# A list scheduler's table of durations corrected from a trace, in an fp32 network kernel on one core

## The chip, the cores and the metric

The kernel runs on one core of a Trainium2 chip. The metric is the device time of one execution in microseconds (us). A change of about 0.2% (6 us here) is the least that a measurement of this kernel can tell from none.

## The reference, cut to what matters

The input is one sequence of 512 tokens of width 1024, all in float32. Two blocks follow each other. The first has an "even" layer (a 31-tap convolution branch and an RWKV-7 recurrence) and an "odd" layer (attention over the best 128 keys per query). The second has a convolution and pooling mixer, a mixture of 16384 one-row experts (PEER), and a gate. The change bears most on PEER:

```python
s = einsum('thpd,hpkd->thpk', q, sub_keys)         # routing: 8 heads, two halves
sv, si = top_k(s, 16)
top_s, pos = top_k(cand, 16)                       # 16 experts per token and head
eidx = take_along_axis(cidx, pos, axis=-1)
gate = softmax(top_s)
u = take(expert_u, eidx, axis=0)
act = gelu(einsum('thkd,td->thk', u, xb))
v = take(expert_v, eidx, axis=0)
out = einsum('thk,thkd->td', gate * act, v)
```

## The kernel before, in words

Matrix products are made in float32r, as three products of a high and a low part (`product`, L216 to L218): high by high, high weight by low input, low weight by high input. A weight piece is loaded by a transfer that SyncE (SP) issues, ScalarE (ACT) makes its high part (`wh`, L207), and GpSimd (POOL) subtracts it to get the low part (`wl`, L209). In the even layer the low part is made by an adding transfer that GpSimd issues instead (`dl`, L192).

PEER (`peer`, L1182 on) works in three stretches.

- **Routing** (`route`, L1399 on). Eight heads of scores, top-16 searches on VectorE (DVE). Then the *scatter*: for 352 of the 512 tokens, eight at a time (44 steps), the chosen gates are spread over all 16384 experts. A step makes one-hot tiles on VectorE (`o`, L1519, and `ob`, L1522), scales them on ScalarE (L1527) and GpSimd (L1528), multiplies them on TensorE (PE, L1533), and copies the result to `st` (L1536). Eleven stores bring `st` to a table `gs` in HBM (L1537).
- **u products.** One tile per 128 experts: activations times expert_u, through gelu (`u_phase`, L1196 to L1199). Thirty-two of the 128 tiles are made ahead, beside the routing, and kept in HBM (`ga`). A u tile is 8 blocks of three matmuls with 352 columns.
- **V stretch** (L1216 on). For each 128 experts `g4`, a piece of the table, is read (L1227), multiplied with the u tile (L1234), split, and multiplied with expert_v (L1264 to L1266), whose low part `vl` GpSimd makes for six tiles of eight (L1248).

The other 160 tokens take another way: 320 *gathers*, indirect transfers that GpSimd issues (`grow`, L1338), one row of 1024 floats for each of 128 partitions. The first 160 rows go into dot products on VectorE (L1353), the other 160 into a weighted sum (L1369). A gather may stand anywhere from the routing to the end of the V stretch. Its tile has five buffers.

Buffers are shared in time: tiles of the V stretch may be written only when all of the routing's pools are closed. Among these is `wx`, an extra buffer for raw weights (`wrawx`) that u tiles use as long as the routing lasts.

No order is written by hand. `Order` builds the dependency graph of the program, estimates each instruction (`cost`), and runs a list scheduler over it (`run`) for several priorities; the order with the shortest estimated end is imposed on every engine's queue and on SP's transfers. Every engine then works strictly in that order.

Of the kernel before, what the change touches and what calls it, by code (L numbers as in the profile page):

```python
# [1566 lines left out]
class Order:  # L1567
# [4 lines left out]
    SETS = {"Exp": (0, 6), "Tanh": (0, 2, 18), "Ln": (5, 6), "Silu": (18,), "Sigmoid": (2,), "Sin": (18,),  # L1572
            "Gelu_apprx_tanh": (11,)}
    LOAD, SWITCH, LANES = 1283, 4000, 8
    TICK, BUSY = 10240 / 3, 3060
    SHAPE = 94

    def __init__(self, nc):
# [15 lines left out]
    def cost(self, i):  # L1594

        e, op = str(i.engine).split(".")[1], str(i.opcode)
        ins = [a for a in i.ins if hasattr(a, "ap")]
        out = list(i.outs)

        def size(a):  # L1600
            return math.prod(c for _, c in list(a.ap)[1:])

        def psum(a):
            return self.mem.get(a.memref, ("",))[0] == "PSUM"
        if "DMA" in op and e == "Pool":
            return e, 0, 1038, 0, 4 * math.prod(c for _, c in out[0].ap)
        if "DMA" in op:
            run = min(list(a.ap)[-1][1] if list(a.ap)[-1][0] == 1 else 1 for a in ins + out)
            return e, 0, 450 if run >= 128 else 625, 0, 4 * math.prod(c for _, c in out[0].ap) * (1 if run >= 128 else 2)
        if op == "LoadActFuncSet":  # L1610
            return e, 0, self.LOAD, 0, 0
        n = max([size(a) for a in ins + out])
        if e == "PE":
            n = size(out[0])
            rows, cols = i.tile_size
            self.shape[i.name] = rows, cols
            one = n / 2.4
            self.col[i.name] = n * rows / 128
            if i.tile_position[1]:
                return e, cols / 1.2, 20, 20, 0  # L1620
            p = 2 if i.is_transpose else 1 if str(i.ins[0].dtype).endswith("float32r") and n >= 256 else 4
            self.col[i.name] *= p
            return e, cols / (2.4 if i.is_transpose else 1.2), p * one + 2.5, one, 0
        sc = sum(size(a) == 1 for a in ins) if n > 1 else 0
        big = [a for a in ins if size(a) > 1]
        if e == "Activation":
            acc = len(out) > 1
            return e, 0, n / 1.2 + (51 if psum(ins[0]) else 93) + 93 * (sc + acc), 0, 0
        if e == "DVE":
            if op == "Memset":  # L1630
                return e, 0, n / 0.96 + 8, 0, 0
            fast = op in ("TensorScalarPtr", "TensorCopy") and len(big) < 2 and not any(map(psum, ins))
            return e, 0, (n / (2 if fast else 1) + 66 + 60 * sc) / 0.96, 0, 0
        if op == "Memset":
            return e, 0, n / 1.2 + 36, 0, 0
        return e, 0, n * (2.1 if len(big) > 1 else 3.3) + 150, 0, 0
# [113 lines left out]
    def run(self, pri):  # L1750
        c, use, dep = self.c, self.use, self.dep
# [18 lines left out]
        soon = {e: [] for e in self.HOP}  # L1770
        now = {e: [] for e in self.HOP}
        lanes, cols, ring, dma, array, table, shape = [], {}, 0.0, 0.0, 0.0, None, None
        out = []

        def push(n):
# [5 lines left out]
        def done(n):  # L1781
            wait[n] -= 1
            if not wait[n]:
                push(n)
# [3 lines left out]
        while len(out) < len(self.seq):  # L1788
            t, e = min((free.get(e, 0) if now[e] else max(free.get(e, 0), soon[e][0][0]), e)
                       for e in soon if now[e] or soon[e])  # L1790
            while soon[e] and soon[e][0][0] <= t:
                _, k, n = heapq.heappop(soon[e])
                heapq.heappush(now[e], (-pri[n], k, n))
            if e == "Activation":
                b = min(now[e], key=lambda z: z[0] + (self.SWITCH if self.fn[z[2]] and table not in self.fn[z[2]] else 0))
                now[e].remove(b)
                heapq.heapify(now[e])
                n = b[2]
            elif e == "PE":
                b = min(now[e], key=lambda z: z[0] + (self.SHAPE if self.shape[z[2]] != shape else 0))  # L1800
                now[e].remove(b)
                heapq.heapify(now[e])
                n = b[2]
            else:
                n = heapq.heappop(now[e])[2]
            _, load, d, last, size = c[n]
            if self.fn[n] and table not in self.fn[n]:
                table = self.fn[n][0]
                t += self.LOAD
            start[n] = t  # L1810
            if size and e == "Pool":
                free[e] = t + d + 3
                dma = end[n] = max(dma, t + d + 650) + size / 360
            elif size:
                if len(lanes) >= self.LANES:
                    t = max(t, lanes[-self.LANES] + 900)
                ring = max(t, ring) + d
                dma = max(dma, ring + 650) + size / 360
                free[e], end[n] = ring, dma
                lanes.append(dma)  # L1820
            elif e == "PE":
                k = int(max(array, t) / self.TICK)
                slow = 1 if cols.get(k - 1, 0) >= self.BUSY else 2
                d += self.SHAPE if self.shape[n] != shape else 0
                shape = self.shape[n]
                array = end[n] = max(array, t + load * slow) + d * slow
                free[e] = array - last * slow + 3
                k = int(array / self.TICK)
                cols[k] = cols.get(k, 0) + self.col[n]
            else:  # L1830
                end[n] = t + d
                free[e] = end[n] + 3
            out.append(n)
            for m in self.succ[n]:
                done(m)
            seen = set()
            for tl in holds.get(n, ()):
                tleft[tl] -= 1
                if not tleft[tl] and queue[self.tag[tl]]:
                    w = first[queue[self.tag[tl]].pop(0)]  # L1840
                    extra[w] = max([extra.get(w, 0)] + [end[x] + self.hop(x, w) for x in use[tl]])
                    done(w)
                p = self.mem[tl][3]
                if p not in seen:
                    seen.add(p)
                    pleft[p] -= 1
                    if not pleft[p]:
                        te = max(end[x] for x in members[p]) + 150
                        for q in self.over[p]:
                            for t2 in self.pools[q]:  # L1850
                                w = first[t2]
                                extra[w] = max(extra.get(w, 0), te)
                                done(w)
# [59 lines left out]
```

## Time and profile before

| | |
|---|---|
| time, median of 3 runs | 2848.27 us (2845.97 to 2852.17) |
| the profiled execution's own time | 2844.42 us |
| its span, first to last instruction | 2842.7 us |
| mean granted TensorE clock | 0.965 of 2.4 GHz |
| TensorE busy with matmuls | 2609.6 us, 92% |
| VectorE, GpSimd, ScalarE busy | 2154.0, 1724.6, 1481.2 us |
| read from and written to HBM | 507.76 and 41.42 MB |

The profile is one execution, so a sum of its durations is to be set against 2844.42 us, of which 1.7 us lie outside the span; the median of the runs is 3.9 us above it. Even layer, odd layer and mixer take the first half of the span, PEER runs from about 1400 us to 2766 us, and the last gate follows.

### The profile page before, as it was taken

Reading aid. Unit: us, or ns where it says so; the run is one execution under the profiler, and the core shown is the slowest. Engines: PE = TensorE matmul, PEld = TensorE weight load, DVE = VectorE, ACT = ScalarE, POOL = GpSimd, SP = SyncE. Lnnn points to the kernel's source line nnn. Section 1 sums busy time; section 2 is a strip of 40 time slices with the busy share of each in tenths; the row PEclk is TensorE's granted clock in tenths of the full one; section 3 lists DMA queues with packets and bytes.
Section 4 is the critical chain, followed back from the end, with each engine's and each line's share of the span. In section 5 each row is a group of like instructions: output and inputs, shape, how many; then the busy total and the mean of one; then the engine's idle time right before and its main releaser. Section 6 shows DMA issues by size and latency. Waiting matters only on the chain. (4 is left out here: it accounts for less than half of the span.)

```text
span 2842.7 us, 45654 instructions
## 1 busy us (share of the span) xinstructions
PE 2609.6 (92%) x14715; PEld 2220.0 (78%) x14715; DVE 2154.0 (76%) x4307; ACT 1481.2 (52%) x3177; POOL 1724.6 (61%) x1870
## 2 busy tenths in 40 slices
PE   5889999999798899999999987779999999999996
PEld 3656667666576688887888777779999999999995
DVE  6686669865379998954669999667877787787875
ACT  6646557568455358965353367424334333344435
POOL 4423523222164443346657788779988888899973
PEclk9889899999899999999999999989999999999998
DMA  8744355555872221223334356889999999999972
GB/s 260 172 96 97 82 117 119 103 145 122 216 241 91 71 80 46 71 84 106 92 111 141 107 193 251 293 299 326 338 321 334 334 337 335 309 334 330 336 253 80
DMA packets 353444, 552.27 MB, mean 194 GB/s; under 512 B 60082, under 2 KB 239154, under 8 KB 351539
## 3 DMA queue, kind: packets, MB, share of 16 engines
q1 hardware_dynamic: 224690, 295.22, 32.2%
q0 software_dynamic: 64800, 201.88, 23.9%
q10 hardware_dynamic: 63712, 52.24, 5.8%
q8 instruction: 116, 1.90, 0.3%
q14 instruction: 126, 1.02, 0.1%
HBM read 507.76 MB, written 41.42 MB: 193 GB/s over the span
## 5 line engine op out<-in xcount | busy, mean ns | idle before, releaser
L209 POOL TENSOR_TENSOR wl<-wraw,wh 128x256 fp32r<-128x256 f32 x937 | 748.3, 816 | 395.8 <-ACT wh L207 314.8
L207 ACT ACTIVATE wh<-wraw 128x256 fp32r<-128x256 f32 x937 | 363.0, 411 | 422.0 <-PE mm L217 198.2
L216 PE MATMUL mm<-xh,wh 128*128 128x352 f32 (+1 forms) x1464 | 513.2, 352 | 32.4 <-ACT wh L207 17.4
L218 PE MATMUL mm<-xh,wl 128*128 128x352 f32 (+1 forms) x1464 | 510.6, 352 | 18.8 <-POOL wl L209 18.8
L217 PE MATMUL mm<-xl,wh 128*128 128x352 f32 (+1 forms) x1464 | 510.5, 350 | 2.3 <-DVE xl L287 2.3
L216 PEld LDWEIGHTS mm<-xh,wh 128*128 128x128 f32 x1464 | 280.5, 192 | 57.2 <-ACT wh L207 21.0
L218 PEld LDWEIGHTS mm<-xh,wl 128*128 128x128 f32 x1464 | 280.5, 192 | 42.1 <-POOL wl L209 24.5
L217 PEld LDWEIGHTS mm<-xl,wh 128*128 128x128 f32 x1464 | 280.8, 192 | 23.3 <-DVE xl L287 4.6
L192 POOL DMA_DIRECT2D dl<-in_wev x114 | 100.7, 904 | 284.1 <-ACT dl L191 261.3
L1248 POOL TENSOR_TENSOR vl<-vraw,vh 128x1024 fp32r<-128x1024 f32 x96 | 230.9, 2407 | 4.0 <-ACT vh L1244 3.0
L1369 DVE SCALAR_TENSOR_TENSOR wide<-grow,gdot,wide 128x1024 f32<-128x1024 f32 x158 | 202.4, 1281 | 17.1 <-DMA grow<-in_ev,gidx 15.9
L218 PE MATMUL mm<-xh,dl 128*128 128x512 f32 x456 | 197.0, 436 | 15.5 <-DMA dl<-in_wev 15.5
L1353 DVE SCALAR_TENSOR_TENSOR gscr<-grow,wide 128x1024 bf16<-128x1024 f32 x160 | 194.1, 1213 | 19.4 <-DMA grow<-in_ue,gidx 18.1
L1199 ACT ACTIVATE mm<-mm 128x352 f32<-128x352 f32 x96 | 43.0, 448 | 314.4 <-PE mm L218 308.5
L216 PE MATMUL mm<-xh,dh 128*128 128x512 f32 x456 | 193.4, 428 | 13.0 <-ACT xh L355 12.3
L1338 POOL DMA_INDIRECT grow<-in_ue,gidx x160 | 164.2, 1026 | 57.8 <-DVE gscr L1353 20.2
L217 PE MATMUL mm<-xl,dh 128*128 128x512 f32 x456 | 191.1, 422 | 6.2 <-DVE xl L356 6.2
L1338 POOL DMA_INDIRECT grow<-in_ev,gidx x160 | 162.6, 1016 | 42.8 <-issue 18.1
L1244 ACT ACTIVATE vh<-vraw 128x1024 fp32r<-128x1024 f32 x128 | 134.4, 1054 | 83.2 <-DMA vraw<-in_ev 70.5
L1264 PE MATMUL xu<-wwh,vh 128*128 128x352 f32 x512 | 167.0, 326 | 5.2 <-DVE x L1268 2.6
L1266 PE MATMUL xu<-wwh,vl 128*128 128x352 f32 x512 | 166.1, 326 | 4.6 <-POOL vl L1248 2.6
L1265 PE MATMUL xu<-wwl,vh 128*128 128x352 f32 x512 | 165.8, 324 | 0.0
(582 smaller groups left out, 6818.7 us busy)
## 6 DMA issues: line engine op xcount, KB each, us to landing
vraw<-in_ev SPq DMA_DIRECT2D x128, 512.0 KB, 5.7
wraw<-in_uT SPq DMA_DIRECT2D x494, 128.0 KB, 4.7
draw<-in_wev SPq DMA_DIRECT2D x114, 256.0 KB, 3.4
dl<-in_wev POOLq DMA_DIRECT2D x114, 256.0 KB, 4.7
gs<-st SPq DMA_DIRECT2D x11, 2048.0 KB, 7.7
g<-gs ACTq DMA_DIRECT2D x32, 704.0 KB, 10.3
wraw<-in_wod SPq DMA_DIRECT2D x156, 128.0 KB, 2.2
adaw<-in_adaT SPq DMA_DIRECT2D x32, 512.0 KB, 8.1
```

The source lines that it names most:

```text
L207: nc.scalar.activation(wh, raw[:, s], AF.Copy)
L209: nc.gpsimd.tensor_tensor(wl, raw[:, s], wh.bitcast(F32), OP.subtract)
L216: nc.tensor.matmul(ps, wh, xh, start=start, stop=False)
L217: nc.tensor.matmul(ps, wh, xl, start=False, stop=False)
L218: nc.tensor.matmul(ps, wl, xh, start=False, stop=stop)
L1248: nc.gpsimd.tensor_tensor(l, raw, h.bitcast(F32), OP.subtract)
L1264: nc.tensor.matmul(po, vh[i][:, s], wh[i], start=(i == 0), stop=False)
L1265: nc.tensor.matmul(po, vh[i][:, s], wl[i], start=False, stop=False)
L1266: nc.tensor.matmul(po, vl[i][:, s], wh[i], start=False, stop=(i == len(wh) - 1))
L1338: self.nc.gpsimd.indirect_dma_start(out=t, out_offset=None, in_=src, in_offset=bass.IndirectOffsetOnAxis(ap=self.gidx[i][:, k:k + 1], axis=0))
L1353: nc.vector.scalar_tensor_tensor(scr, u, 1.0, x, op0=OP.mult, op1=OP.mult, accum_out=self.gdot[i][:, k:k + 1])
L1369: nc.vector.scalar_tensor_tensor(acc, r, w, acc, op0=OP.mult, op1=OP.add)
```

## The change

Nothing in the program changes, only `Order`'s estimates, and with them the order in which each engine gets its instructions.

- An adding transfer on GpSimd is taken as 920 ns of issue in place of 1038, and as 10 bytes per element for the transfer engines in place of 4.
- A one-pass matmul costs 15 ns over its columns in place of 2.5.
- VectorE work with two operands in SBUF, or in its fast mode, takes 1.25 times as long per element.
- The model of TensorE's clock gets two thresholds, one to rise and one to fall, and keeps its state between them.

```diff
-    TICK, BUSY = 10240 / 3, 3060
+    TICK, BUSY, FULL = 10240 / 3, 4000, 7200
+    PORT = 1.25
...
-            return e, 0, 1038, 0, 4 * math.prod(c for _, c in out[0].ap)
+            add = str(out[0].dtype).endswith("float32r")
+            return e, 0, 920 if add else 1038, 0, (10 if add else 4) * math.prod(c for _, c in out[0].ap)
...
-            return e, cols / (2.4 if i.is_transpose else 1.2), p * one + 2.5, one, 0
+            return e, cols / (2.4 if i.is_transpose else 1.2), p * one + (15 if p == 1 else 2.5), one, 0
...
-            return e, 0, (n / (2 if fast else 1) + 66 + 60 * sc) / 0.96, 0, 0
+            port = fast or sum(not psum(a) for a in big) > 1
+            return e, 0, (n / (2 if fast else 1) * (self.PORT if port else 1) + 66 + 60 * sc) / 0.96, 0, 0
...
-                slow = 1 if cols.get(k - 1, 0) >= self.BUSY else 2
+                while tick < k:
+                    c2 = cols.get(tick, 0)
+                    slow = (1 if c2 >= self.FULL / 2 else 2) if slow == 2 else 2 if c2 < self.BUSY else 1
+                    tick += 1
```

What this does to the order is spread over the even layer, the start of the odd one, and PEER. Counted in the two orders, on GpSimd's and VectorE's queues:

| | before | changed |
|---|---|---|
| dot products (L1353) ahead of the first one-hot step / of the last | 8 / 16 | 0 / 6 |
| gathers ahead of the last L1528 of the scatter | 21 | 11 |
| gathers ahead of the 1st, 49th, 61st, 79th, 85th `vl` (L1248) | 39, 188, 222, 267, 285 | 23, 168, 205, 266, 285 |
| `wl` (L209) between first and last L1528 | 23 | 36 |
| u blocks on TensorE between first and last L1533 | 35 | 68 |
| u blocks between the last L1533 and the first V matmul | 66 | 28 |

The first place is GpSimd's queue around the end of the scatter; `o0` are the scatter's steps, `grow` gathers, `wl` low parts of expert_u. Before, from the last two steps on:

```order
L1528 TENSOR_TENSOR o0_18738<-ob_18736,kt_18505 128x512
L209 TENSOR_TENSOR wl_19566<-wrawx_19562,wh_19564 128x256
L1528 TENSOR_TENSOR o0_18760<-ob_18758,kt_18505 128x512
L1338 DMA grow_17165<-in_ue,gidx0_14978 128x1024
...
L1338 DMA grow_18952<-in_ue,gidx0_14978 128x1024
L1338 DMA grow_18956<-in_ue,gidx0_14978 128x1024
L209 TENSOR_TENSOR wl_19770<-wrawx_19766,wh_19768 128x256
```

Between the last step and the last use of `wrawx` (`wl_19770`) stand 26 instructions, 13 of them gathers. Now the same `wl_19770` stands ten steps ahead of the last:

```order
L1528 TENSOR_TENSOR o0_18536<-ob_18534,kt_18505 128x512
L209 TENSOR_TENSOR wl_19770<-wrawx_19766,wh_19768 128x256
L1528 TENSOR_TENSOR o0_18558<-ob_18556,kt_18505 128x512
...
L1528 TENSOR_TENSOR o0_18738<-ob_18736,kt_18505 128x512
L1528 TENSOR_TENSOR o0_18760<-ob_18758,kt_18505 128x512
L1338 DMA grow_16287<-in_ue,gidx0_14978 128x1024
L209 TENSOR_TENSOR wl_19908<-wraw_19904,wh_19906 128x256
```

The weights moved ahead of the steps, the gathers behind them. The second place is VectorE's queue at the start of the scatter (`gscr` are dot products, `sel`, `sm` and `top` the end of the routing). Before:

```order
L1353 SCALAR_TENSOR_TENSOR gscr,gdot_14976<-grow,wide 128x1024
L1320 SCALAR_TENSOR_TENSOR gsrc<-sel 128x16 x3
L1322 COPY gidx_14978<-gsrc 128x16 x3
...
L1353 SCALAR_TENSOR_TENSOR gscr,gdot_14976<-grow,wide 128x1024
L1499 TENSOR_REDUCE sm<-sel 128x32
L1353 SCALAR_TENSOR_TENSOR gscr,gdot_14976<-grow,wide 128x1024
L1500 RECIPROCAL sm<-sm 128x32
...
L1353 SCALAR_TENSOR_TENSOR gscr,gdot_14976<-grow,wide 128x1024
L1320 SCALAR_TENSOR_TENSOR gsrc<-sel 128x16 x2
L1519 TENSOR_TENSOR o_17774<-iota,kt 128x1024
```

Now:

```order
L1495 TENSOR_TENSOR sel<-sel,top 128x512
L1322 COPY gidx_14978<-gsrc 128x16
L1320 SCALAR_TENSOR_TENSOR gsrc<-sel 128x16
L1499 TENSOR_REDUCE sm<-sel 128x32
L1500 RECIPROCAL sm<-sm 128x32
L1501 TENSOR_TENSOR sel<-sel,sm 128x512
L1379 COPY gate_17758<-sel 128x128
L1519 TENSOR_TENSOR o_17774<-iota,kt 128x1024
```

The dot products are gone from ahead of the first step. The third place is TensorE's queue in the even layer, at the first triangular solve (L686, 32x32). Before it stands behind projections (`mm<-xh,dh`) and among the next head pair's products (L626):

```order
L216 MATMUL mm<-xh_103,dh 128x512
L217 MATMUL mm<-xl_111,dh 128x512
L218 MATMUL mm<-xh_103,dl 128x512
L686 MATMUL xu<-T_1433,MT 32x32
L626 MATMUL tp<-AR,BK 128x128 x8
L686 MATMUL xu<-T_1433,MT 32x32
L626 MATMUL tp<-AR,BK 128x128 x4
```

Now it stands in one piece among the convolution's products (`uh`, `sg`), ahead of the projections that it stood behind:

```order
L217 MATMUL mm<-sg,pr 128x512
L218 MATMUL mm<-uh,pr 128x512
L216 MATMUL mm<-uh,pr 128x512
L686 MATMUL xu<-T_1433,MT 32x32 x16
L217 MATMUL mm<-sg,pr 128x512
L218 MATMUL mm<-uh,pr 128x512
L644 MATMUL tp<-con,v 128x128 x4
```

Other head pairs' solves and recurrence steps move by about as much, some ahead and some back; from 700 us to 950 us, and from 1200 us to 1500 us, the two orders differ by a few instructions only.

## Rows read from the trace of the kernel before

**Rows 1.** Windows, PEER: length; busy PE, PEld, DVE, ACT, POOL (instructions); clock, DMA share, GB/s.

```profile
1873.00:2440.00 567.00, 553.06 (x3361) 545.44 (x3360) 429.13 (x697) 219.82 (x475) 502.52 (x485) 0.99 0.96 329
2440.00:2600.00 160.00, 157.75 (x974) 156.87 (x973) 128.46 (x163) 66.90 (x138) 144.52 (x136) 1.00 0.94 323
1563.00:1668.00 105.00, 92.29 (x485) 83.14 (x484) 105.00 (x487) 40.17 (x100) 76.29 (x94) 0.94 0.42 130
1668.00:1806.00 138.00, 110.40 (x830) 101.08 (x828) 134.74 (x117) 110.66 (x295) 115.71 (x81) 1.00 0.62 232
1806.00:1873.00 67.00, 41.90 (x201) 38.07 (x201) 29.72 (x48) 16.83 (x41) 42.02 (x49) 0.77 0.92 322
```

**Rows 2.** The chain that ended last, around the start of the V stretch (start us, us).

```profile
1834.86 0.75 POOL wl L209
...
1835.63 0.43 ACTq L1227
...
1836.16 21.08 DMA g<-gs
...
1873.02 0.19 PE xu L1264
```

**Rows 3.** Waits between 1806 and 1873 us: total us, times, longest us.

```profile
PE mm L216 <- ACT wh L207: 15.9, 2, 14.1
PE mm L218 <- POOL wl L209: 9.2, 4, 3.9
```

**Rows 4.** VectorE and GpSimd lines of the routing and gathers: ns min/median/max, first and last start us.

```profile
L1353 DVE SCALAR_TENSOR_TENSOR gscr<-grow,wide x160: 1203/1211/1223, 1644.2 to 2245.6; 128x1024 bf16<-128x1024 f32 x160
L1519 DVE TENSOR_TENSOR o<-iota,kt x44: 1210/1214/3854, 1665.8 to 1802.1; 128x1024 f32<-128x1024 f32 x44
L1522 DVE TENSOR_TENSOR ob<-keys,kb x44: 677/1525/3281, 1666.9 to 1798.4; 128x1024 bf16<-128x1024 bf16 x44
L209 POOL TENSOR_TENSOR wl<-wraw,wh x94: 718/737/1784, 1601.5 to 1900.0; 128x256 fp32r<-128x256 f32 x94
```

**Rows 5.** Groups of the whole span: busy us, mean ns of one, idle before.

```profile
L1519 DVE TENSOR_TENSOR o<-iota,kt 128x1024 f32<-128x1024 f32 x44 | 69.3, 1576 | 0.3 <-PE xu L1533 0.3
L1522 DVE TENSOR_TENSOR ob<-keys,kb 128x1024 bf16<-128x1024 bf16 x44 | 59.5, 1360 | 2.9 <-POOL o L1528 2.9
L1338 POOL DMA_INDIRECT grow<-in_ue,gidx x160 | 164.2, 1026 | 57.8 <-DVE gscr L1353 20.2 <-issue 16.2 <-DVE pf L1469 5.6
```

**Rows 6.** DMA issues from 1700 to 1900 us: KB each, median us to landing.

```profile
gs<-st SPq DMA_DIRECT2D x9, 2048.0 KB, 7.7
g<-gs ACTq DMA_DIRECT2D x3, 704.0 KB, 12.2
```

**Rows 7.** All transfers of the table `gs`.

```profile
L1537 SPq DMA_DIRECT2D gs<-st x11: 320/326/546, 1680.9 to 1806.9; - x11
DMA to landing us min/median/max: 5.4/9.7/21.1
```

**Rows 8.** The first steps of the V stretch: ns min/median/max.

```profile
L1234 DVE TENSOR_TENSOR mm<-mm,g x96: 518/532/533, 1867.0 to 2746.4; 128x352 f32<-128x352 f32 x96
L241 ACT ACTIVATE wwh<-mm x90: 441/464/468, 1872.1 to 2694.0; 128x352 fp32r<-128x352 f32 x90
```

**Rows 9.** TensorE in time, even layer: start us, us, idle before and releaser.

```profile
164.29 0.79 PE L218 MATMUL mm<-xh,dl 128*128 128x512 f32 x1 [5.07 <-DMA dl<-in_wev]
165.01 0.31 PE L686 MATMUL xu<-T,MT 32*32 32x32 f32 x2
```

**Rows 10.** The solve's input, VectorE's transposes in the even layer up to 260 us.

```profile
L681 DVE STREAM_TRANSPOSE T<-Tt x6: 426/432/432, 159.1 to 234.1; 32x256 f32<-32x256 f32 x6
```

**Rows 11.** A window of the even layer, columns as in rows 1.

```profile
150.00:178.00 28.00, 22.93 (x128) 18.33 (x126) 22.42 (x51) 11.16 (x24) 8.53 (x16) 0.73 0.56 116
```

## What the change will do

> **What bounds the kernel now.** Start with the windows over PEER [rows 1]. In the V stretch, 1873 to 2600 us, TensorE is busy 553.06 of 567 us and 157.75 of 160 us at a clock of 0.99 to 1.00: it is the bound, and a matmul comes every 553.06 / 3361 = 0.165 us. Two others are nearly as full: GpSimd 502.52 of 567 us, the transfer engines 0.96 and 0.94. No reordering can make that work shorter; it can only start earlier or be held up. So look at what lies ahead of it. From 1563 to 1806 us VectorE is busy 105.00 of 105 and 134.74 of 138 us, while TensorE idles 12.7 and 27.6 us: the end of the routing and the scatter are bound by VectorE. From 1806 to 1873 us nobody is full: TensorE 41.90 of 67 us at a clock of 0.77, VectorE 29.72, GpSimd 42.02. That stretch is waiting.
>
> The chain of waits says for what [rows 2]. The first V matmul starts at 1873.0 us, behind a 21.08 us read of the table (`g<-gs`), which ScalarE issued at 1835.6 us, right behind a `wl` that GpSimd ran at 1834.86 us. By the program's names that is `wl_19770`, the last use of `wrawx`. The last store of the scatter went out at 1806.9 us [rows 7], so for 20 us and more the table was there and unread: the buffers of the V stretch were closed until a u tile's leftover weight was done, and that stood on GpSimd behind 13 gathers. In this stretch TensorE itself waits for weights, 15.9 us for `wh` and 9.2 us for `wl` [rows 3].
>
> **The change, step by step.** The sums go against the profiled execution, 2844.4 us; the median of the runs is 3.9 us higher.
>
> *Routing and scatter.* Ten dot products of 1.211 us [rows 4] leave VectorE's queue ahead of the last one-hot step (16 before, 6 now): 10 x 1.211 = 12.1 us off the engine that is the bound. Against that, GpSimd gets 13 more `wl` and 3 fewer gathers beside the scatter, 89 instructions for 79. The one-hot steps take 1210 ns at least but 1576 on average, and 677 at least but 1360 on average [rows 4, 5]: (366 + 683) x 44 = 46 us of lengthening beside those 79. In proportion ten more cost 46 x 10 / 79 = 5.8 us. I take 5: the step is worth **-7 us**. Its ends are -12 (no lengthening) and -2.5 (every added `wl`, 13 x 0.737 us, holds VectorE in full). The 33 u blocks that now stand in the scatter cost TensorE 33 x 3 x 0.165 = 16 us, which its 27.6 idle us hide; GpSimd's 13 x 0.737 us are hidden by its 22 idle us [rows 1]. Were that cover gone, 16 us of the gain would go.
>
> The Trainium skill (SBUF — State Buffer, "Who interferes with whom") says that a VectorE instruction with two SBUF inputs and a GpSimd instruction that reads SBUF exclude each other for a whole instruction, while a VectorE instruction with at most one SBUF input does not contend. By that rule the added `wl` would be paid in full and this step would be worth -2.5 us, not -7, and the time 4.5 us more, which lies within the forecast's own range. The trace agrees in kind: dot products, whose other input is in PSUM, spread by 20 ns only, the one-hot steps by 2.6 us [rows 4].
>
> *Start of the V stretch.* `wl_19770` now stands ten steps ahead of the scatter's end, so the buffers open when the last store is out. What remains from there: 0.9 us to the store, 7.7 us to its landing, 12.2 us for the read [rows 6], 0.53 and 0.46 us to multiply and split [rows 8]: 22 us. Beside it TensorE has 28 u blocks to do (66 before): 84 x 0.165 = 14 us, or 28 us at the 1.2 GHz which it had for part of this stretch. I take 30 us in place of 67, since idle waiting is what lowered the clock there: **-37 us**. Ends: with every transfer at the 9.7 us median of this table and the full clock, 20 us (-47); with the read at its longest, 21.1 us [rows 7], and one wait for weights of 14.1 us [rows 3] on top, 47 us (-20).
>
> *V stretch.* As many u blocks are done at its start as before, but 16 gathers fewer (23 for 39). The lag stays to the 49th `vl` (168 for 188) and is made up between the 61st and the 79th: 61 gathers where there were 45. Where the lag is constant nothing changes. In the catch-up, near 2440 to 2600 us, GpSimd gets 16 x 1.026 = 16.4 us more [rows 5] and has 15.5 us idle [rows 1]: +1 us. The transfers get 16 rows of 0.52 MB, 8.4 MB, at 323 GB/s 26 us, with 6% of 160 = 9.6 us idle: +16 us. The ends are 0 and +26. I take **+13**, nearer the transfers' row, because gathers and weight loads share those engines and TensorE has only a few buffers of reserve.
>
> *Even layer.* The first solve is moved ahead by 13 us of TensorE work. It started at 165.0 us, behind a 5.07 us wait for a `dl` [rows 9]; its input was ready at about 160 us [rows 10]. So the move can cost some 7 us of waiting for that input, or give back the 5 us. The window is slow as it is, clock 0.73, TensorE 22.93 of 28 us [rows 11]. Later moves go both ways, and the layer's last 50 us are in the same order. I take **0**, with 10 us either way. The moves at the start of the odd layer I cost at nothing: they exchange work that all of TensorE has to do.
>
> Sum: -7 - 37 + 13 + 0 = -31 us, 2813.4 us for a profiled execution, **2817 us** for the median.
>
> **The rivals.**
> - *The catch-up spreads.* If the transfers, not TensorE, carry the V stretch, all 26 us of the later gathers come back: -7 - 37 + 26 = -18, 2830 us. For it: the share of 0.96. Against it: TensorE's 0.98 at full clock.
> - *Another wait takes the gate's place.* The scatter grows by its added weights (-2.5 and 16 us of TensorE work uncovered, +13.5), the start takes 47 us (-20), the catch-up 10: +3.5 us, about 2850 us, no change that can be told. For it: the waits for weights [rows 3] and that all engines of the scatter are then over 85% full. Against it: the weights come from SP's queue with room ahead.
> - *The clock falls in the catch-up*, the slower end. If TensorE waits there again and again, it may get the clock of the stretch before the V products, 0.77 [rows 1]: 160 us of matmuls then take 160 / 0.77 = 208 us. With the waits themselves, 13 us, that is +61 against -44: 2865 us. It decides once the catch-up costs over 44 + 6 = 50 us in all. Against it: from 2440 to 2600 us the clock stood at 1.00 with the transfers at 0.94.
> - The orders do differ at the places that count, so a change without any effect is only a coincidence of sizes, and is in the second rival.
>
> **How the numbers follow.** Forecast 0.60, catch-up spread 0.13, another wait 0.14, clock 0.10; 0.03 for an even layer that loses 35 us or more. An effect under about 0.2%, 6 us, can't be told from none. The forecast and the first rival are faster: 0.73. Of the second rival 0.13 is within 0.2% and 0.01 slower; with the clock and the even layer that makes 0.14 slower. The likeliest case alone runs from 2798 us (the start at -47, the catch-up at +4: -50) to 2838 us. The range for 8 in 10 goes on to the second rival: 2797 to 2853 us.
>
> **What would show it.** In the changed profile: the first `vl` (1859.1 us before) and the first V matmul some 40 us earlier; no `wl` ahead of the table's read in the chain; the window between the scatter's end and the V stretch down from 67 to about 30 us; VectorE full up to the scatter's end, with dot products behind it; and a dent, with TensorE waiting for `wl`, `vh` or `wh`, some 600 us into the V stretch. I am wrong if the first V matmul is less than 20 us earlier, if the V stretch grows by more than 26 us, or if the even layer's end moves by more than 10 us.

## The result, and the profile after

The changed kernel takes 2952.04 us (median of 3 runs, 2948.37 to 2957.49) where the kernel before takes 2848.27: a ratio of 1.0367, 95% interval 1.0343 to 1.0390. It is 104 us slower. The forecast was 2817 us, and its range ended at 2853 us.

The page of the changed kernel, its span and its first row (the table of before has 2842.7 and 2609.6 us, and a clock of 0.965; the clock of this run is 0.941):

```profile
span 2950.3 us, 45755 instructions
...
PE 2643.6 (90%) x14715; PEld 2242.5 (76%) x14715; DVE 2190.9 (74%) x4307; ACT 1489.6 (50%) x3178; POOL 1726.2 (59%) x1870
```

The work is the same, yet TensorE needs 34 us more for it and stands idle for longer. To see where, set milestones of both traces side by side (start of the instruction named, us):

| | before | changed | the stretch that ends there |
|---|---|---|---|
| first product of the even layer's output projection | 782 | 838 | even layer +56 |
| `I-13306`, a product late in the odd layer's output projection | 1292 | 1368 | odd layer +20 |
| first routing product (the mixer is done, PEER begins) | 1455 | 1535 | mixer +4 |
| last scatter product (L1533) | 1806 | 1885 | routing and scatter -1 |
| first V product (L1264) | 1873 | 1916 | start of the V stretch -36 |
| last V product | 2765 | 2874 | V stretch +66 (892 to 958) |

Runs with the same order in a stretch repeat it within some 9 us. So the forecast's largest gain, the start of the V stretch, came in the size that was forecast, and three stretches that it had at nothing or little (even layer, odd layer, V stretch) lost 142 us. The windows over PEER, which answer to [rows 1]:

```profile
1639.00:1746.00 107.00, 94.20 (x525) 86.29 (x523) 104.45 (x492) 43.02 (x105) 81.73 (x101) 0.98 0.42 127
1746.00:1885.00 139.00, 120.58 (x914) 113.54 (x914) 137.81 (x101) 115.70 (x311) 124.42 (x91) 1.00 0.64 235
1885.00:1916.00 31.00, 13.54 (x85) 13.25 (x83) 14.44 (x26) 8.90 (x21) 19.98 (x24) 0.77 1.03 360
1916.00:2395.00 479.00, 447.91 (x2679) 439.51 (x2680) 378.92 (x613) 184.58 (x384) 419.32 (x396) 0.98 0.95 328
2395.00:2874.00 479.00, 447.89 (x2691) 440.04 (x2689) 355.60 (x466) 173.51 (x355) 391.35 (x376) 0.97 0.87 301
```

The same window over the whole V stretch of the kernel before:

```profile
1873.00:2765.00 892.00, 875.79 (x5363) 866.99 (x5361) 687.53 (x1034) 349.37 (x742) 791.20 (x757) 0.99 0.94 324
```

The stretch of waiting between scatter and V is 31 us in place of 67. But in the V stretch TensorE is busy 895.80 of 958 us, before 875.79 of 892: 62 us idle for 16, and 20 us more of busy time for the same products at a clock of 0.97 to 0.98 in place of 0.99. That is the whole +66.

The chain around the start, which answers to [rows 2] (start us, us):

```profile
1885.95 11.52 DMA gs<-st
1897.56 15.95 DMA g<-gs
1913.63 0.54 DVE ga L1234
1914.17 0.87 DVE mm L1234 x2
1915.05 0.87 DVE wwl L242 x2
```

No `wl` stands ahead of the read (`g<-gs`) any more. The read is issued as soon as the last store has landed.

Where TensorE now stops in the V stretch (waits from 1916 to 2874 us: total us, times, longest):

```profile
PE xu L1264 <- DVE x L1268: 26.2, 18, 4.6
...
PE nb L1264 <- DVE x L1268: 12.9, 6, 5.2
PE xu L1266 <- POOL vl L1248: 12.0, 8, 3.7
```

The same waits in the kernel before, from 1873 to 2765 us:

```profile
PE xu L1266 <- POOL vl L1248: 2.6, 3, 1.4
PE xu L1264 <- DVE x L1268: 2.6, 4, 1.4
...
PE nb L1264 <- DVE x L1268: 0.8, 1, 0.8
```

And what VectorE, which is late with that `x`, stands for in the same stretch:

```profile
DVE wide L1369 <- DMA grow<-in_ev,gidx: 69.5, 49, 5.8
```

In the kernel before:

```profile
DVE wide L1369 <- DMA grow<-in_ev,gidx: 15.9, 13, 5.3
```

### The profile page after: what moved, and what is told of

The parts are those of the page before. It is cut to its first block, busy times and chain, and to the rows that moved or that the text cites. A ratio compares the mean times of both kernels' runs of the same rounds, so it can differ in the third digit from the quotient of the medians.

```text
span 2950.3 us, 45755 instructions
## 1 busy us (share of the span) xinstructions
PE 2643.6 (90%) x14715; PEld 2242.5 (76%) x14715; DVE 2190.9 (74%) x4307; ACT 1489.6 (50%) x3178; POOL 1726.2 (59%) x1870
## 4 chain that ended last, share of the span: by engine, by line
PE 36%; DVE 13%; DMA 9%; issue 3%; POOL 3%; ACT 2%; SPq 0%; ACTq 0%; DVEq 0%; POOLq 0%
PE mm L217 7%; PE mm L218 7%; PE mm L216 7%; DMA grow<-in_ev,gidx 3%; DMA g<-gs 3%; PE xu L1266 2%; PE xu L1264 2%; PE xu L1265 2%; DMA wraw<-in_uT 1%; DVE wide L1369 1%; POOL wl L209 1%; PE tp L1040 1%; DVE stmp L1428 1%; PE nb L1264 1%; PE tp L1266 1%
## 5 line engine op out<-in xcount | busy, mean ns | idle before, releaser
L209 POOL TENSOR_TENSOR wl<-wraw,wh 128x256 fp32r<-128x256 f32 x937 | 754.5, 821 | 474.6 <-ACT wh L207 338.3
L207 ACT ACTIVATE wh<-wraw 128x256 fp32r<-128x256 f32 x937 | 374.4, 414 | 595.8 <-PE mm L217 387.2
L216 PE MATMUL mm<-xh,wh 128*128 128x352 f32 (+1 forms) x1464 | 512.3, 351 | 47.1 <-DVE ropet L878 23.9
L1369 DVE SCALAR_TENSOR_TENSOR wide<-grow,gdot,wide 128x1024 f32<-128x1024 f32 x158 | 203.0, 1285 | 70.5 <-DMA grow<-in_ev,gidx 69.5
L1248 POOL TENSOR_TENSOR vl<-vraw,vh 128x1024 fp32r<-128x1024 f32 x96 | 230.6, 2409 | 7.1 <-ACT vh L1244 6.3
L216 PE MATMUL mm<-xh,dh 128*128 128x512 f32 x456 | 200.2, 441 | 17.5 <-ACT xh L355 7.0
L1353 DVE SCALAR_TENSOR_TENSOR gscr<-grow,wide 128x1024 bf16<-128x1024 f32 x160 | 194.3, 1214 | 28.9 <-DMA grow<-in_ue,gidx 26.0
L217 PE MATMUL mm<-xl,dh 128*128 128x512 f32 x456 | 198.5, 436 | 10.6 <-DVE xl L356 10.6
L1264 PE MATMUL xu<-wwh,vh 128*128 128x352 f32 x512 | 171.2, 334 | 30.3 <-DVE x L1268 26.2
L1338 POOL DMA_INDIRECT grow<-in_ue,gidx x160 | 157.7, 986 | 51.2 <-issue 17.5
L790 DVE SCALAR_TENSOR_TENSOR x<-u,vec,x 128x512 f32<-128x512 f32 x184 | 143.3, 780 | 5.7 <-ACT x L788 3.4
```

The costliest lines, as they stand in the source:

```text
L207: nc.scalar.activation(wh, raw[:, s], AF.Copy)
L209: nc.gpsimd.tensor_tensor(wl, raw[:, s], wh.bitcast(F32), OP.subtract)
L216: nc.tensor.matmul(ps, wh, xh, start=start, stop=False)
L217: nc.tensor.matmul(ps, wh, xl, start=False, stop=False)
L1248: nc.gpsimd.tensor_tensor(l, raw, h.bitcast(F32), OP.subtract)
L1264: nc.tensor.matmul(po, vh[i][:, s], wh[i], start=(i == 0), stop=False)
```

## The experiments

Fourteen runs. Their times stand beside one run each of the kernel before on the same chip (2845.71 us for the three parts and the 15 ns alone, 2852.28 for the thresholds alone, the 1.25 alone, the transfer rate and the refitted table, 2849.78 as the median of seven for the lower thresholds, the fixed tile and the joined order, 2841.23 for the other three). Except for the joined order each was run once; they are read by milestones of the trace.

### Which place loses what

Three kernels take the changed order in one place and the old one elsewhere. `joined` lists the instructions of one table's order up to a named one, and then what is left in the other's order; `Old` is `Order` with the entries of before. `I-7740` is the first product of the even layer's output projection. `I-13306` is the first product of the seventh of the eight tiles of the odd layer's output projection. (The expectations call it the middle of that projection, and in one place the first PEER product; but in the kernel before the first PEER product comes 163 us later, behind the mixer.) What is given below as "from `I-13306` on" is therefore the end of the odd layer, the mixer and PEER.

```diff
-    nc = build(A, Order(build(A)).best()[1])
+    nc = build(A, joined(build(A), ((Order, 'I-7740'), (Old, None))))
```

> The changed order up to the first product of even_out, the order of before from there on. If each place loses by its own order (theory 1), the even layer's 55 us come and nothing else: about 2903 us against 2848. If the even layer's loss came from a state of the chip in that one execution or is made up behind it (rival), 2848 to 2860 us.

Measured: 2897.26 us, +51.6.

```diff
+    nc = build(A, joined(build(A), ((Old, 'I-7740'), (Order, 'I-13306'), (Old, None))))
```

> The changed order in the odd layer alone, between the first product of even_out and the middle of the odd layer's output product; before on both sides. Theory 1: the 22 us that the changed profile loses between 925 and 975 us, about 2870 us. Rival (the loss there is inherited from the late even layer): 2848 to 2853 us.

Measured: 2869.89 us, +24.2. The place can be named. Waits of TensorE for the rope step from 783 to 1000 us in this run:

```profile
PE mm L216 <- DVE ropet L878: 23.9, 1, 23.9
```

And from 782 to 1000 us in the kernel before:

```profile
PE mm L216 <- DVE ropet L878: 10.9, 3, 8.4
```

One product at the head of TensorE's queue waits for a rope step (L878), and VectorE, which makes it, is full with the searches of the attention (L985, L986). This is a place where the two orders were said to differ by a few instructions only. A window of this run shows it, VectorE busy throughout, TensorE for 26 of 60 us and at a mean clock of 0.66:

```profile
911.00:971.00 60.00, 26.46 (x83) 18.00 (x82) 59.87 (x127) 14.88 (x27) 6.89 (x10) 0.66 0.07 22
```

The kernel before at the same place:

```profile
910.00:970.00 60.00, 47.37 (x193) 35.95 (x192) 59.75 (x123) 22.84 (x48) 20.99 (x28) 0.91 0.19 59
```

```diff
+    nc = build(A, joined(build(A), ((Old, 'I-13306'), (Order, None))))
```

> The order of before up to the middle of the odd layer's output product, the changed order from there on (mixer, routing, scatter, V stretch). Theory 1: the V stretch starts about 45 us earlier than before and takes about 65 us longer, 2868 to 2875 us. Rival (the V stretch lost because of what came ahead of it): 2805 to 2820 us, as predicted.

Measured: 2877.77 us, +32.1, 3 us over the expected range. The V stretch starts 34 us earlier than before, at 1839 us, and is 961 us long. The three parts sum to 108 us, and the whole change cost 104: the places add, and each can be studied by itself.

### Which entry of the table

The table of before with only the 15 ns of a one-pass matmul:

```diff
-            return e, cols / (2.4 if i.is_transpose else 1.2), p * one + 2.5, one, 0
+            return e, cols / (2.4 if i.is_transpose else 1.2), p * one + (15 if p == 1 else 2.5), one, 0
```

> The table of before with one edit alone: 15 ns over its columns for a one-pass matmul. Theory A (the true TensorE time takes the slack out of the schedule, in which GpSimd, transfers and hops are still too short): the V stretch loses as in the changed kernel, 2890 to 2960 us in all. Rival B (the other three edits are to blame): 2830 to 2860 us.

Measured: 2901.47 us, +55.8. The even layer ends at 790 us (782), the V stretch takes 949 us (892). So this entry alone lengthens PEER; the 8 us of the even layer are no more than runs of one order differ by.

The table of before with only the thresholds (and the state kept between them):

```diff
-    TICK, BUSY = 10240 / 3, 3060
+    TICK, BUSY, FULL = 10240 / 3, 4000, 7200
...
-                slow = 1 if cols.get(k - 1, 0) >= self.BUSY else 2
+                while tick < k:
+                    c2 = cols.get(tick, 0)
+                    slow = (1 if c2 >= self.FULL / 2 else 2) if slow == 2 else 2 if c2 < self.BUSY else 1
+                    tick += 1
```

> The table of before with only the two thresholds of TensorE's clock. Theory A (the thresholds are too high: the scheduler sees a slow clock in the even layer where the chip has the full one, and pays to avoid it): the even layer ends 40 to 80 us later than before (its first product of the output projection), and the time is 2836 + 46 to 76 = 2882 to 2912 us. Rival (the even layer's loss comes from the adding transfers' 10 bytes instead): the even layer ends within 15 us of before, and the time is within 2835 to 2865 us.

Measured: 2916.22 us, 4 us over the range of theory A. With the thresholds alone the even layer ends at 825 us, 43 us late, as theory A has it.

The other way round, the changed table with lower thresholds:

```diff
-    TICK, BUSY, FULL = 10240 / 3, 4000, 7200
+    TICK, BUSY, FULL = 10240 / 3, 2500, 6400
```

> The changed table with lower thresholds for the clock alone (2500 and 6400 for 4000 and 7200), everything else as changed. If the thresholds cost the even layer its time: its end (first product of the output projection, 782 us before, 838 with the change) is back at 765 to 800 us, and the time is some 40 to 60 us under the changed kernel's, 2885 to 2915 us, with PEER as long as with the change. If the adding transfers' 10 bytes did it: the even layer still ends after 815 us, and the time is 2925 us or more.

Measured: 2841.85 us, below what was expected, and by one run no different from the kernel before. The even layer ends at 761 us, with the adding transfers' 10 bytes left in; from there to `I-13306` it takes 495 us (before 510, changed 530). From `I-13306` to the last V product it takes as long as with the change, 1502 us (changed 1506, before 1473), though not in the same places: the V stretch takes 936 us (changed 958), and the routing and scatter 375 (changed 350). The even layer from 60 us to its end, of the kernel before:

```profile
60.00:782.00 722.00, 651.69 (x4121) 464.42 (x4120) 495.06 (x1101) 439.15 (x926) 239.85 (x346) 0.93 0.57 127
```

of the changed kernel:

```profile
60.00:838.00 778.00, 682.58 (x4108) 485.01 (x4108) 503.02 (x1103) 433.98 (x922) 238.58 (x342) 0.87 0.53 118
```

with the thresholds alone:

```profile
60.00:825.00 765.00, 672.67 (x4109) 476.44 (x4109) 501.15 (x1096) 434.07 (x922) 238.37 (x343) 0.90 0.53 120
```

and with lower ones in the changed table:

```profile
60.00:761.00 701.00, 640.83 (x4108) 457.89 (x4106) 494.26 (x1097) 432.32 (x922) 238.34 (x342) 0.94 0.58 131
```

The same 4,100 matmuls take 31 us more busy time in the changed kernel, at a mean clock of 0.87 for 0.93, and TensorE stands still for 95 us in place of 70. (A mean of 0.87 between the two levels, 1.2 and 2.4 GHz, is a quarter of the stretch at the lower one, 0.93 a seventh.) The thresholds describe the clock to the scheduler, and the order made with them lowered it. With lower ones, clock and idle time are better than before. This is shown by both directions: put in alone they cost 43 us in the even layer, lowered in the changed table they give back 77. The last run still keeps the state between them, so it is their height that costs.

The table of before with only VectorE's 1.25:

```diff
+    PORT = 1.25
...
-            return e, 0, (n / (2 if fast else 1) + 66 + 60 * sc) / 0.96, 0, 0
+            port = fast or sum(not psum(a) for a in big) > 1
+            return e, 0, (n / (2 if fast else 1) * (self.PORT if port else 1) + 66 + 60 * sc) / 0.96, 0, 0
```

> The table of before with only the 1.25 on VectorE's work beside GpSimd. The refitted durations put this order at 2733 + 46 to 76 = 2779 to 2809 us, faster than before. Theory C (any new order loses): 2880 us or more. Theory A needs only that it is no worse than before by more than 10 us.

Measured: 2840.38 us. The even layer ends at 758 us, `I-13306` is reached at 1254 us (before 1292), and from there to the last V product it takes 1501 us (before 1473). Expected were 2779 to 2809, and this is a miss for the estimate; theory C, any new order at 2880 us or more, misses as well, and theory A's own condition, no worse than before by more than 10 us, holds.

### What lengthens the V stretch

The changed table with a lower rate of the transfer engines (in `length` too):

```diff
-                dma = end[n] = max(dma, t + d + 650) + size / 360
+                dma = end[n] = max(dma, t + d + 650) + size / 335
...
-                dma = max(dma, ring + 650) + size / 360
+                dma = max(dma, ring + 650) + size / 335
```

> The changed table with one more correction: the transfer engines are taken at 335 bytes per ns, about what the V stretch moved in every trace so far (327 to 334 GB/s at a share of 0.93 to 0.97), in place of 360. Theory A (the V stretch lost its time to transfers that the table thinks faster than they are: with TensorE's products now at their true length the scheduler believes that the transfers have slack, and puts them late): the first V matmul comes as early as with the change or later, but the V stretch, 65 us longer with the change than before, is back within 25 us of before, and the time is 2846 to 2870 us, with the even layer's loss largely still there. Theory B (the u products stand too late in TensorE's queue, whatever the transfers do; or waits between engines are too short in the table): the V stretch keeps 40 us or more of its 65, and the time is 2900 us or more.

Measured: 2920.75 us, the V stretch 950 us. Theory A failed here, and theory B's numbers came. Most of the gain on the changed kernel is in the even layer, which ends at 809 us (changed 838). The waits for gathered rows on VectorE fell to 3.1 us, and TensorE's for `vl` took their place. TensorE from 1878 to 2828 us in this run:

```profile
PE xu L1266 <- POOL vl L1248: 32.2, 24, 3.3
...
PE xu L1264 <- DVE x L1268: 11.2, 7, 2.5
```

The changed table with the entries refitted to the traces:

```diff
-    TICK, BUSY, FULL = 10240 / 3, 4000, 7200
+    TICK, BUSY, FULL = 10240 / 3, 2500, 6400
...
-            add = str(out[0].dtype).endswith("float32r")
-            return e, 0, 920 if add else 1038, 0, (10 if add else 4) * math.prod(c for _, c in out[0].ap)
+            return e, 0, 1038, 0, 4 * math.prod(c for _, c in out[0].ap)
...
-                dma = end[n] = max(dma, t + d + 650) + size / 360
+                dma = end[n] = max(dma, t + d + 2500) + size / 335
...
-                dma = max(dma, ring + 650) + size / 360
+                dma = max(dma, ring + 1500) + size / 335
```

(335 stands in `length` too, and 1.25 and the 15 ns stay as changed.)

> The changed table with every duration as the six traces so far fit it best: transfers at 335 bytes per ns, landing 1500 ns (hardware queues) and 2500 ns (GpSimd's) in place of 650 ns after issue, adding transfers as before the change, and lower thresholds for TensorE's clock (2500 and 6400 for 4000 and 7200). Replayed with these durations, the six orders that ran come out 46 to 76 us below their measured times, evenly enough to rank them. Theory A (the losses come from entries of the table that are wrong by the traces: thresholds too high in the even layer, transfers too fast in PEER): the order made with them is faster than both kernels, about 2688 + 46 to 76 = 2734 to 2764 us. Theory C (any new order loses, since the old one was hit on by chance and the model is too coarse to rank orders): 2880 to 2950 us, as the two new orders so far.

Measured: 2844.90 us, 81 us or more over what theory A expected, and 35 us or more under theory C. The gain came early and was lost again behind: the even layer ends at 736 us and `I-13306` is reached at 1234 us, 58 us before the old order; the V stretch then takes 969 us, and again TensorE waits for `vl`, here from 1791 to 2759 us:

```profile
PE xu L1266 <- POOL vl L1248: 25.0, 24, 3.0
PE mm L218 <- POOL wl L209: 16.4, 16, 2.6
```

Does VectorE's waiting for gathered rows matter at all? In the next kernel the PEER order is the changed one, and the dot products (L1353) and sums (L1369) read a fixed tile, so that VectorE doesn't wait for a row (the 160 tokens' use of the rows is left out):

```diff
-                nc.vector.scalar_tensor_tensor(scr, u, 1.0, x, op0=OP.mult, op1=OP.mult,
+                nc.vector.scalar_tensor_tensor(scr, self.xtok[1] if STILL else u, 1.0, x, op0=OP.mult, op1=OP.mult,
...
                 r = self.rows(v, i, k)
+                r = self.xtok[1] if STILL else r
```

> The run with the changed order in PEER alone (V stretch 961 us, 892 before), where the 160 tokens' dot products and weighted sums read a fixed tile in place of the gathered rows; all gathers are still issued and move their bytes, but VectorE never waits for one to land (this part of the output is left wrong, and it is left out of the computation). Theory D (VectorE stands in front of gathers that the order puts too close ahead of their use, and TensorE then waits for VectorE's x): the V stretch falls to 920 us or less, the time to 2840 us or less. Theory A (the transfer engines are full, whoever waits for them): the V stretch stays at 945 us or more, the time at 2860 us or more.

Measured: 2852.24 us, and the V stretch 928 us: between the two theories. The control, the same edit under the old order:

> The order of before with the fixed tile alone (full rows; left out of the computation: the 160 tokens' use of the rows), the control for the run with a fixed tile. Theory D (landing waits cost only where the order puts gathers close ahead of their use, and the old order does not: 15.9 us of such waits on VectorE against 69.5 us): V stretch 885 to 892 us. If it falls by as much as with the changed order (33 us), the waits cost both orders alike and do not tell them apart.

Measured: 2839.67 us, the V stretch 889 us. So with nothing to wait for the changed order gains 33 us and the old one 3, which is no more than runs of one order differ by. The edit also lets GpSimd issue a gather without waiting until VectorE has read its buffer, so the gain could come from there. Against that speak TensorE's waits. In the run with the changed PEER order and gathered rows (1839 to 2800 us) they are

```profile
PE xu L1264 <- DVE x L1268: 25.3, 20, 3.6
...
PE nb L1264 <- DVE x L1268: 13.6, 6, 9.0
PE xu L1266 <- POOL vl L1248: 11.6, 9, 3.3
```

and with the fixed tile (1846 to 2773 us)

```profile
PE xu L1264 <- DVE x L1268: 15.0, 11, 3.5
PE xu L1266 <- POOL vl L1248: 11.9, 7, 3.8
PE nb L1264 <- DVE x L1268: 3.2, 3, 2.0
```

What TensorE waits for from VectorE falls, and what it waits for from GpSimd stays.

For what is left, the gathers' bytes were cut to a quarter as well:

```diff
-        self.nc.gpsimd.indirect_dma_start(out=t, out_offset=None, in_=src, in_offset=bass.IndirectOffsetOnAxis(
+        self.nc.gpsimd.indirect_dma_start(out=t[:, :256] if STILL else t, out_offset=None, in_=src.rearrange("a (b c) -> (a b) c", c=256) if STILL else src, in_offset=bass.IndirectOffsetOnAxis(
```

> As the run before it with a fixed tile in place of the gathered rows (V stretch 928 us), and each gather now fetches a quarter of a row, 256 floats, so that the gathers' bytes fall to a quarter while GpSimd issues as many (left out of the computation: the 160 tokens' use of the rows, and three quarters of each row). The transfer engines should be some 60 to 75% busy. Theory A (the rest of the V stretch's growth, 928 - 892 = 36 us, is transfers that are full): V stretch 880 to 905 us. Theory B (it is the order on TensorE and GpSimd and the clock that waiting brings): 918 to 935 us.

> The same two edits, a fixed tile and a quarter of each row, under the order of before everywhere (V stretch 892 us): the control. TensorE had 16 us without work in this stretch, so all that waiting can give back is some 16 us: V stretch 876 to 890 us under either theory. If it falls below 870 us, the products themselves were slowed by the transfers.

Measured: 2835.13 us with a V stretch of 923 us under the changed order, 2826.08 us and 887 us under the old one. The two halves of each V stretch, columns as in [rows 1]. The changed PEER order:

```profile
1839.00:2319.00 480.00, 450.60 (x2687) 441.82 (x2687) 374.90 (x612) 184.24 (x385) 419.93 (x395) 0.98 0.94 327
2319.00:2800.00 481.00, 445.77 (x2683) 436.58 (x2682) 355.42 (x466) 172.68 (x354) 393.56 (x377) 0.98 0.87 301
```

with a fixed tile:

```profile
1845.00:2309.00 464.00, 441.51 (x2629) 434.93 (x2629) 363.18 (x600) 178.76 (x372) 410.68 (x384) 0.97 0.94 328
2309.00:2773.00 464.00, 450.22 (x2736) 444.38 (x2735) 361.58 (x477) 179.65 (x366) 404.82 (x388) 0.99 0.92 322
```

with a fixed tile and a quarter of each row:

```profile
1833.00:2295.00 462.00, 440.45 (x2647) 433.20 (x2648) 370.26 (x605) 178.80 (x375) 414.89 (x388) 0.98 0.66 205
2295.00:2756.00 461.00, 445.44 (x2720) 441.14 (x2719) 358.40 (x471) 179.19 (x364) 405.51 (x385) 0.99 0.62 193
```

and the same two edits under the old order:

```profile
1858.00:2315.00 457.00, 444.34 (x2707) 438.61 (x2706) 349.44 (x589) 174.58 (x382) 408.71 (x391) 0.99 0.65 204
2315.00:2745.00 430.00, 428.13 (x2657) 426.86 (x2655) 344.74 (x447) 172.99 (x361) 390.92 (x365) 1.00 0.64 201
```

With the transfer engines at 0.62 to 0.66, the changed order is still 36 us longer than the old one. So full transfers are not what holds it (theory B): with their share down by a third the stretch is 5 us shorter, no more than runs of one order differ by. TensorE idles 37 us under the changed order and 15 us under the old one (sums of the columns), and its products take 13 us longer. What it stops for is VectorE's `x` and GpSimd's `vl`, as with the fixed tile alone. Which moves of the order put them late there stays open; no run separates them.

The traces do show how the orders differ on GpSimd, which issues the gathers and makes the `vl`. Pair each gather with the weighted sum (L1369) that reads its row, and each of GpSimd's `vl` with the first product that uses it. In the old order a sum starts 9.4 us after its gather's issue, and a product 3.8 us after its `vl` is done (medians). The orders of the changed table, of the 15 ns alone and of the lower thresholds have the gathers closer, 7.7 to 8.3 us, and the `vl` farther ahead, 11.7 to 16.9 us. The orders of the thresholds alone, of the 1.25 alone, of the lower rate and of the refitted table have it the other way round, 11.0 to 11.7 us and 0.3 to 1.4 us. All seven take 931 to 969 us for the V stretch. So a table that cures VectorE's waits for rows need not cure the stretch: it moved them to `vl`.

### A version that beats both

```diff
+class Fit(Order):
+    PLAIN = True
+    RATE, LAND, LATE = 335, 1500, 2500
+    BUSY, FULL = 2500, 6400
...
+    nc = build(A, joined(build(A), ((Fit, 'I-13306'), (Old, None))))
```

(`PLAIN` leaves the adding transfers as before the change; `RATE`, `LAND` and `LATE` replace 360 and the two 650.)

> The order of the run with all durations refitted, up to the first PEER product on TensorE, and the order of before from there. That run reached the first PEER product at 1234 us (before 1292 us) but took 1525 us from there to the last V matmul (before 1473). If places add, as they did for the change, and the old PEER order is as good behind an earlier start: 58 us less than before, 2785 to 2805 us. If PEER's length hangs on what was moved ahead of it in the old order: 2825 us or more.

Measured: 2795.99 us (median of 4 runs, 2789.12 to 2803.18), a ratio of 0.9814 to the kernel before, 95% interval 0.9782 to 0.9845. Even layer, from `I-13306` to the first V product, V stretch:

```profile
60.00:741.00 681.00, 634.89 (x4105) 455.10 (x4103) 494.24 (x1096) 430.47 (x917) 241.74 (x339) 0.95 0.59 135
1239.00:1818.00 579.00, 506.83 (x2740) 440.28 (x2739) 462.37 (x1260) 300.81 (x726) 413.41 (x440) 0.96 0.50 169
1818.00:2718.00 900.00, 877.38 (x5365) 866.75 (x5364) 687.36 (x1034) 351.56 (x743) 796.81 (x757) 0.99 0.94 321
```

The refitted table gives 53 us up to `I-13306`, and the old order keeps its length behind the earlier start: 1479 us from there to the last V product, before 1473.

## Why the prediction was wrong

- **Start of the V stretch, -37 us (-47 to -20): the wait was right, the size in part luck.** The window is 36 us shorter, and the chain is the one that was named: no `wl` ahead of the read. But the 30 us that were taken for it came from TensorE's 28 u blocks at the low clock. TensorE was busy for 13.54 us only, and waited once, 17.5 us for the first `wwl`. What filled the stretch were the store and the read, 11.52 and 15.95 us where 7.7 and 12.2 were taken.
- **Routing and scatter, -7 us (-12 to -2.5): not there, -1 us.** Ten dot products did leave VectorE ahead of the last step, 12.1 us. But the one-hot steps lengthened by more than the 5 us taken, [rows 4, 5] against:

```profile
L1519 DVE TENSOR_TENSOR o<-iota,kt 128x1024 f32<-128x1024 f32 x44 | 77.6, 1784 | 1.0 <-ACT kt L1512 0.9
...
L1522 DVE TENSOR_TENSOR ob<-keys,kb 128x1024 bf16<-128x1024 bf16 x44 | 60.6, 1402 | 2.0 <-POOL o L1528 2.0
```

  Their means rose by 208 and 42 ns: 250 x 44 = 11 us, which eats the 12. That GpSimd's added work beside them lengthened them fits, but no run separates it from the rest of the order. The rule that was cited from the Trainium skill (SBUF — State Buffer, "Who interferes with whom"), by which every added `wl` is paid in full (13 x 0.737 = 9.6 us), was nearer to this than the proportion that I took from the trace.
- **V stretch, +13 us (0 to +26), "where the lag is constant nothing changes": the step that failed in PEER.** It grew by 66 us, some 20 in the first half of its products and 45 in the second, where I had allowed only a catch-up of 61 gathers. I counted gathers against `vl`, that is how much work moves, and priced it by busy time and bytes. What the order changed was how close ahead of its use each thing stands: a sum now starts 8.1 us after its gather's issue in place of 9.4 (medians), and 44 of 160 sums under 7 us in place of 20, while the rows land 6.9 us after issue. Of the 69 us in the run with PEER alone, 33 went when VectorE had no rows to wait for and 5, within the noise, with the transfers' load. The rest are TensorE's waits for `x` and `vl` and longer products at a slightly lower clock; which moves made them stays open. The rival of full transfers named the right stretch and a wrong cause; its 26 us were too few. No single entry is at fault either: from `I-13306` to the last V product the old order takes 1473 us, the tables with the 15 ns, the thresholds or the 1.25 alone 1521, 1505 and 1501 us, the lower rate 1503, the refitted one 1525. With the thresholds or the 1.25 alone much of this is in routing and scatter already, 379 and 370 us where the old order takes 351. And an early start of the V stretch was worth nothing in any order that ran: from the last scatter product to the last V product the old order took 959 us, the eight other complete kernels that start the stretch within 50 us of the scatter's end (the PEER part alone and the changed table among them) 963 to 1005.
- **Even layer, 0 us (10 either way), from one move of 13 us looked at in detail: failed, +56.** That the other moves "go both ways" was said without working them out. The clock's two thresholds did it, 43 us when put in alone, 77 us back when lowered, by a clock of 0.87 for 0.93 and 25 us more of standing still. I gave a loss of 35 us or more 3 chances in 100.
- **"The moves at the start of the odd layer I cost at nothing: they exchange work that all of TensorE has to do": failed, +20.** One product waits for a rope step, and TensorE stands 23.9 us behind it, where all such waits had come to 10.9.
- **The clock** fell, as the third rival had it, but in the even layer and at the stop in the odd one. The V stretch had 0.97 to 0.98, not 0.77.
- **The scheduler's own view.** Run through the scheduler's own model with the order held fixed, the old order ends at 2531 us by the old table and at 2856 by the changed one, and the chip's span is 2843; the changed order ends at 2770 by the changed table, and the chip's span is 2950. The new numbers describe the old order far better. But the search took an order for which its own table was too hopeful by 180 us. One of its entries that was wrong: a gather of 0.52 MB lands there after 650 ns and 1456 ns for its bytes (at 360 bytes per ns), on the chip 6.9 us after its issue:

```profile
grow<-in_ev,gidx POOLq DMA_INDIRECT x160, 6.9
```

  Correcting that entry, in the refitted table, did not mend PEER: VectorE's waits for these rows went down to 11.4 us, and TensorE's for `vl` came, 25.0 us.

## What to carry to other kernels

A table that predicts the time of the present order better need not rank orders better: the search moves into the entries that are still wrong, so test a correction by the order it makes, entry by entry and place by place (joining two orders at a milestone showed here with three runs that the losses add). When an order is moved, don't price only the bytes and busy time that move: look for each instruction at how far ahead of its use its input stands, since an engine as full as TensorE here, 98% of the V stretch before, has no reserve for a wait. And keep what each order does well: the joined order beat both.

## What the runs showed that I had not expected

TensorE's clock over the even layer ranged from 0.87 to 0.96 with the order alone (0.96 in the run with all entries refitted, 60 to 736 us), and the busy time of the same products from 683 to 629 us with it. And a third of the transfer engines' load could be taken away in the V stretch, 0.94 to 0.65, for only 2 to 5 us, no more than runs of one order differ by.
